# A block with four mixers on one core: value products of the first mixer for four blocks at a time, prefix tiles in its running sum, another order of the weights

## The chip, the cores and the metric

The kernel runs on one core of a Trainium2 chip. The metric is the device time of one execution in microseconds (us); the median over several runs is compared.

## The reference

One transformer-like block over a sequence of 512 tokens of width 1024, all in float32. `x` is normalised and projected by `w_in` to 6,440 columns, which four mixers of width 512 share:

```python
h = _rmsnorm(x, norm_g)
p_fox, p_ssm, p_nsa, p_mem = _split(h @ w_in, ...)
mem_kv = _rmsnorm(mem, mem_norm_g) @ w_mem_kv
o = concat([_fox_mixer(p_fox, ...), _ssd_mixer(p_ssm, ...),
            _nsa_mixer(p_nsa, ...), _mem_mixer(p_mem, mem_kv)])
return _rmsnorm(x + o @ w_out, final_norm_g)
```

- fox (the first mixer): causal attention with 8 heads of 64; to the scores it adds the difference of a running sum over time of the log of a forget gate, `c = cumsum(log_sigmoid(f_logit + f_bias))`; the output is multiplied by a gate.
- ssd (the second): a state-space mixer in four chunks of 128 tokens, behind a convolution over four steps and with a gated norm.
- nsa (the third): attention with compressed, selected and windowed keys, 8 heads in two groups, with a bias by distance.
- mem (the fourth): attention over 256 memory tokens, 4 heads of 128.

## The kernel before

The program is written out by a planner while it is built: Python objects count an estimated clock for each engine, and the order in which instructions are issued follows from it. On the chip the order is fixed.

**The stream of projections.** `ORDER` (line 42) lists 76 weight tiles of 128x1024. Each is loaded by one DMA on SP's queue (the first by two) into a ring of three raw tiles, split by ACT into a rounded high part `wh` and by `tt` (line 500) on DVE or POOL into a low part `wl`; a product in high precision is three matmuls, high by high, high by low and low by high (`three`). `tt` gives the work to DVE only if its estimated end there plus a handicap (`SOON`, `LATER`, `WIDE`) is earlier than on POOL. The first seven tiles (`bv`, `bc`) hold the values and small columns of all four token blocks (`proj_b`, line 554); while the last ones run, the input is normalised. Every further tile of the list is a generator (`tile_a`, line 663, for a projection into the tile `pj`; `out_proj` and `out_last`, lines 824 and 854, for the products with `w_out` into `po`) that stops after every three matmuls. The list is served strictly in order, and `ready` (line 627) says whether its head may start: there must be room in the pools of tiles (`gs`, 51 tiles of 512 columns, and `bs`, 12 of 1024), and an output projection `wo0`, `wo1`, `wo2` needs all four parts of its mixer's output.

**The pipes.** The mixers are pipes of stages (`Pipe`, line 319): `fox` (line 971), `nsa` (1175), `ssm` (1365) and `mem` (1571), with `compress` ("cmp") and `prep` ("pre") as preparations. A step of `fox` or `nsa` is a head pair j and a block b of 128 queries (in `nsa` also a half a); its stages are scores and softmax (s1, tiles `pS`, `pF`, `pN`), transposes (s2, `pT`, `pt`), value products (s3, `pO`) and the gate (s4). `DF, DM, DN, DS` (line 25) say how many steps of a pipe may be in flight, and for each stage a pipe names the PSUM banks and the tiles that it needs. `Sched.run` (line 237 and on) looks at the first `ACTIVE` unfinished pipes in the order of `PIPES`, issues a stage whose data are ready by the estimated clock, and fills PE with the next three matmuls of the list where none is. If the list is blocked, the earliest stage is issued though its data are late.

**The clock.** `Clock.note` (line 123) estimates each instruction. Matmuls of plain fp32 into at most 64 columns use half of the array; between them and all others the estimate adds 100 ns at each change, in either direction.

**The running sum.** `smalls` (line 890) makes the log gates on DVE and writes them into a tile `s4`, four blocks of 128 columns. `fox_bias` (line 925) sums them over time into `pd`: for block t the products of blocks 0 to t-1 with a tile of ones and of block t with a triangle (`U`), which is ten matmuls. A plain fp32 matmul stands as two records in the profile.

**The value products of the first mixer.** In `fox`'s s3 nothing happens for blocks 0 and 2; at block 1 the products of blocks 0 and 1, and at block 3 those of blocks 2 and 3 are issued, into a PSUM tile of which each head of the pair takes 64 rows. The transposed weights (`pt`, one tile of 512 columns for each four blocks of 128 keys of both heads) are held until then.

**The first weight tile.** For the `bv` tiles the six groups of four matmuls (k-half j, part x: 0 high by high, 1 input low, 2 weight low) go in the order (0,0), (0,1), (1,0), (0,2), (1,1), (1,2).

Of the kernel before, what the change touches and what calls it, by code (L numbers as in the profile page):

```python
# [10 lines left out]
FT = mybir.dt.float32  # L11
# [12 lines left out]
NL = 3  # L24
DF, DM, DN, DS = 4, 5, 5, 4
BACKLOG = 3000
RAW, RING = 3, 3
PIPES = "cmp", "fox", "pre", "nsa", "ssm", "mem"
LAST = 3
ACTIVE = 3  # L30

RF, RM, RN, RS = 2, 3, 2, 4

SOON, LATER, WIDE = 500, 2500, 5000

# [6 lines left out]
ORDER = (  # L42
# [14 lines left out]
class Clock:  # L57
# [65 lines left out]
    def note(self, eng, op, a, k):  # L123
# [12 lines left out]
        if eng == "PE":  # L136
# [7 lines left out]
            if tiled != self.tiled:  # L144
                start += 100
                self.tiled = tiled
# [90 lines left out]
class Sched:  # L237
# [53 lines left out]
    def run(self, pipes):  # L291
        self.pipes = pipes = list(pipes)
        while pipes:
# [15 lines left out]
            if best[0] > now:  # L309
                t = self.due()  # L310
                if t <= now or t <= best[0]:
                    if t == math.inf:
                        raise RuntimeError(f"nothing can run: {self.todo[0][0]}, {[p.at for p in pipes]}")
                    self.fill()
                    continue
            best[1].run(self, best[2])

# [42 lines left out]
def block_kernel(ctx, tc, I, out):  # L360
# [26 lines left out]
    def MD(name, w):  # L387
        return sb.tile([128, w], FT, name=name, tag="md", bufs=5)

# [164 lines left out]
    def proj_b(name, n, per, width):  # L554
        pb = [PS("pb") for t in range(4)]
        for i in range(n):
            h_, l_ = get((name, i))
            ks_ = range(i * per, min((i + 1) * per, KT))
            if name == "bv":
                order = [(0, 0), (0, 1), (1, 0), (0, 2), (1, 1), (1, 2)]  # L560
            else:
                order = [(j, x) for j in range(len(ks_)) for x in (0, 1)] + [(j, 2) for j in range(len(ks_))]
# [325 lines left out]
    gat = C1("gat", [128, 4, 24])  # L888

    def smalls():  # L890
        y = SM("y", 64).rearrange("p (t c) -> p t c", t=4)
# [17 lines left out]
        for i in range(4):  # L909
            V.tensor_copy(out=s4f.rearrange("p (t c) -> p t c", t=4)[:, :, 32 * i:32 * i + 8], in_=sp[:, :, 0:8])  # L910
        ea = SM("ea", 8)
        A.activation(ea, v_al, AF.Exp)
# [3 lines left out]
        V.tensor_scalar(out=gat, in0=gat, scalar1=1.0, scalar2=0.5, op0=OP.add, op1=OP.mult)  # L916

    crs = []

# [5 lines left out]
    def fox_bias():  # L925
        s4 = s4f.rearrange("p (t c) -> p t c", t=4)
        p = PS("pd")
        for t in range(4):
            for u in range(t + 1):
                T.matmul(p[:, t * 128:(t + 1) * 128], s4[:, u, :], U if u == t else ones, start=u == 0, stop=u == t)  # L930
        gs.drop()
# [39 lines left out]
    def fox():  # L971
# [28 lines left out]
        def s3(s):  # L1000
            j, b1 = s
            if b1 == 1:
                st["o"] = PS("pO")
            o = st["e", s] = st.get("o")
            for b in (b1 - 1, b1) if b1 % 2 else ():
                pts = st.pop((j, b))
# [168 lines left out]
    def nsa():  # L1175
# [66 lines left out]
        def s3(s):  # L1242
            j, b, a = s
            if a == 0:
                return
            if b == 0 or j == 3 and LAST == 2:
                st["o"] = PS("pO")
            o = st["o"]
            p0, (p1, ct) = [st.pop((j, b, x)) for x in range(2)]
            pa = p0, p1  # L1250
            os_ = [o[64 * x:64 * x + 64, b * 128:(b + 1) * 128] for x in range(2)]
            for x in range(2):
                T.matmul(os_[x], vcm[:, x * 64:(x + 1) * 64], ct[:96], start=True, stop=False)
            for br in range(2):
                for k in range(b + 1):
                    for x in range(2):
                        T.matmul(os_[x], nv[:, k, br * 128 + x * 64:br * 128 + x * 64 + 64], pa[x][br * (b + 1) + k],
                                 start=False, stop=br == 1 and k == b)
            st["e", s] = o
            gs.drop(2 * ((b + 2) // 2))  # L1260

# [66 lines left out]
    def ssm_pre():  # L1328
# [13 lines left out]
        T.matmul(pa[:64, :128], dA2, U, start=True, stop=True)  # L1342
        ar = sb.tile([64, 128], FR, name="ar", tag="md", bufs=5)
        A.copy(out=ar, in_=pa[:64, :128])
# [20 lines left out]
    def ssm():  # L1365
# [147 lines left out]
        def p3(c):  # L1513
            return [("z", j) for j in range(4)], lambda: []

        return Pipe(list(range(4)), [s1, s2, s3, s4, s5], DS, [5, 1, 1, 1, 1], [(2, 0), (1, 0), (2, 0), (0, 0), (3 if LAST == 1 else 1, 0)], RS,
                    {0: p1, 2: p3})
# [157 lines left out]

    bg.until(clock.ready([s4f]))
    cr()
# [116 lines left out]
```

## Time and profile before

| | us |
|---|---|
| median of three runs | 549.83 |
| lowest and highest of them | 547.93, 550.03 |
| the profiled execution | 548.13 |
| its span, first to last instruction | 546.0 |
| TensorE busy | 535.0 (98%) |
| VectorE busy | 326.5 (60%) |
| ScalarE busy | 318.2 (58%) |
| GpSimd busy | 240.1 (44%) |

In the rows below, PE is TensorE's matmuls, PEld its weight loads, DVE VectorE, ACT ScalarE, POOL GpSimd and SP the engine whose queue issues DMAs. Tiles go by the program's names, `out<-in`. Times are from the span's start. Matmuls are pipelined: one lasts longer than the distance to the start of the next, so the pace of a stream is read from starts.

### The profile page before, as it was taken

Reading aid. Unit: us, or ns where it says so; the run is one execution under the profiler, and the core shown is the slowest. Engines: PE = TensorE matmul, PEld = TensorE weight load, DVE = VectorE, ACT = ScalarE, POOL = GpSimd, SP = SyncE. Lnnn points to the kernel's source line nnn. Section 1 sums busy time; section 2 is a strip of 40 time slices with the busy share of each in tenths; the row PEclk is TensorE's granted clock in tenths of the full one; section 3 lists DMA queues with packets and bytes.
Section 4 is the critical chain, followed back from the end, with each engine's and each line's share of the span. In section 5 each row is a group of like instructions: output and inputs, shape, how many; then the busy total and the mean of one; then the engine's idle time right before and its main releaser. Section 6 shows DMA issues by size and latency. Waiting matters only on the chain.

```text
span 546.0 us, 8842 instructions
## 1 busy us (share of the span) xinstructions
PE 535.0 (98%) x3237; PEld 447.8 (82%) x3237; DVE 326.5 (60%) x870; ACT 318.2 (58%) x714; POOL 240.1 (44%) x159
## 2 busy tenths in 40 slices
PE   8999999999999999999999899999999999999995
PEld 5898888887888888888888688888988888888884
DVE  2676678465754536876665755656655576656443
ACT  5755545747766624735553676667666676756333
POOL 3595525325131444767786451133422213055523
PEclk9999999999999999999999999999999999999998
DMA  8774323222441521262326221511421112022113
GB/s 281 303 268 138 116 77 110 83 77 78 141 130 44 199 72 42 100 245 77 116 93 194 76 65 59 161 59 60 155 79 40 68 49 79 1 78 82 73 39 116
DMA packets 18791, 59.01 MB, mean 108 GB/s; under 512 B 2187, under 2 KB 2459, under 8 KB 18748
## 3 DMA queue, kind: packets, MB, share of 16 engines
q1 hardware_dynamic: 18604, 58.19, 31.4%
q8 instruction: 25, 0.41, 0.3%
q10 hardware_dynamic: 144, 0.26, 0.1%
q14 instruction: 18, 0.15, 0.1%
HBM read 55.80 MB, written 4.81 MB: 111 GB/s over the span
## 4 chain that ended last, share of the span: by engine, by line
PE 96%; DMA 1%; ACT 1%; POOL 1%; DVE 0%; SPq 0%; issue 0%; POOLq 0%; ACTq 0%
PE pj L233 47%; PE po L233 16%; PE pO L233 7%; PE pT L233 6%; PE pb L233 6%; PE pS L233 5%; PE pmv L233 2%; PE pW L233 2%; PE pY L233 1%; DMA xt<-in_xT 1%; PE pcm L233 1%; PE pst L233 0%; PE pd L233 0%; PE pR L233 0%; POOL acc L233 0%; PE pG L233 0%
## 5 line engine op out<-in xcount | busy, mean ns | idle before, releaser
L233 POOL TENSOR_TENSOR wl<-raw,wh 128x1024 fp32r<-128x1024 f32 (+1 forms) x72 | 172.1, 2395 | 239.5 <-ACT wh L233 205.8
L233 PE MATMUL pj<-hh,wh 128*128 128x512 f32 x352 | 141.7, 403 | 0.0
L233 PE MATMUL pj<-hh,wl 128*128 128x512 f32 x352 | 137.6, 391 | 0.0
L233 PE MATMUL pj<-hl,wh 128*128 128x512 f32 x352 | 137.4, 390 | 0.0
L233 ACT ACTIVATE wh<-raw 128x1024 fp32r<-128x1024 f32 (+1 forms) x72 | 74.8, 1041 | 14.2 <-DMA raw<-in_wst 8.2
L233 PEld LDWEIGHTS pj<-hh,wl 128*128 128x128 f32 x352 | 66.1, 188 | 14.5
L233 PEld LDWEIGHTS pj<-hh,wh 128*128 128x128 f32 x352 | 66.2, 188 | 12.6 <-issue 1.2
L233 PEld LDWEIGHTS pj<-hl,wh 128*128 128x128 f32 x352 | 66.3, 188 | 11.3
L233 ACT ACTIVATE pN<-pN,nm 128x128 f32<-128x128 f32 (+7 forms) x96 | 45.3, 473 | 29.2 <-DVE nm L233 28.3
L233 PE MATMUL po<-wh,oh 128*128 128x512 f32 x96 | 39.1, 407 | 0.7 <-ACT oh L233 0.7
L233 PE MATMUL po<-wh,ol 128*128 128x512 f32 x96 | 37.6, 392 | 0.6 <-POOL ol L233 0.6
L233 PE MATMUL po<-wl,oh 128*128 128x512 f32 x96 | 37.5, 391 | 0.0
L233 ACT ACTIVATE pN<-pN,rs 128x128 f32<-128x128 f32 (+3 forms) x32 | 18.0, 564 | 25.8 <-DVE rs L233 24.8
L233 DVE CUSTOM_DVE_ANT_0 pN<-pS,bt 128x128 f32<-128x128 f32 (+4 forms) x72 | 21.1, 328 | 18.0 <-PE pS L233 17.7
L233 DVE TENSOR_TENSOR acc<-acc,po 128x512 f32<-128x512 f32 (+1 forms) x33 | 21.2, 666 | 11.1 <-PE po L233 11.0
L233 ACT ACTIVATE pF<-pF,nm 128x128 f32<-128x128 f32 (+3 forms) x32 | 17.8, 556 | 14.3 <-DVE nm L233 14.0
L233 DVE SCALAR_TENSOR_TENSOR xs<-cb,cwh,xs 128x512 f32<-128x512 f32 x24 | 20.7, 861 | 9.0 <-ACT xs L233 8.2
L233 DVE TENSOR_SCALAR rs<-sm 128x3 f32<-128x3 f32 x32 | 8.4, 262 | 28.2 <-ACT pN L233 28.2
L233 PE MATMUL pT<-cst,pN 128*128 128x128 f32 x160 | 23.5, 278 | 1.2 <-ACT pN L233 1.2
L233 ACT COPY pt<-pT 128x512 f32<-128x512 f32 (+1 forms) x43 | 20.6, 485 | 5.8 <-PE pT L233 5.7
L233 PEld LDWEIGHTS pT<-cst,pN 128*128 128x128 f32 x160 | 18.2, 140 | 5.8 <-issue 2.2
L233 PEld LDWEIGHTS po<-wh,ol 128*128 128x128 f32 x96 | 18.0, 188 | 5.0 <-POOL ol L233 1.1
(273 smaller groups left out, 1095.1 us busy)
## 6 DMA issues: line engine op xcount, KB each, us to landing
raw<-in_wst SPq DMA_DIRECT2D x74, 512.0 KB, 3.3
rows<-rv SPq DMA_DIRECT2D x4, 656.0 KB, 7.5
bt<-rows SPq DMA_DIRECT2D x4, 528.0 KB, 4.2
xt<-in_xT SPq DMA_DIRECT2D x8, 256.0 KB, 6.6
xn<-in_xn SPq DMA_DIRECT2D x4, 512.0 KB, 7.8
w<-in_w SPq DMA_DIRECT2D x4, 512.0 KB, 7.2
acc<-in_xn SPq DMA_DIRECT2D x4, 512.0 KB, 5.0
out<-acc SPq DMA_DIRECT2D x7, 256.0 KB, 2.3
```

Source lines behind the costliest of these rows:

```text
L233: return f(*a, **k)
```

## The change

In the first mixer, s3 waits until block `GF - 1` (GF is 4) and issues the products of all four blocks of a head pair in one run; up to eight steps may be in flight. In `smalls`, two adds on DVE make the sums of the first two and the first three blocks of `s4`, in tiles from a pool that grows from five to seven; in `fox_bias` each block then takes one matmul with the triangle and one with ones, seven in all, and the first call waits for these tiles too. The first `bv` tile goes in natural order. The estimate adds 50 ns where a change leads into the half-array matmuls and 220 ns where it leads out. `ssm` comes before `nsa` among the pipes, four of them are looked at, `DM` is 6, `DN` 4, `WIDE` 8000. A stage of `ssm` may ask for three free tiles where it asked for two. When a pipe's best stage has become impossible after the list was looked at, the planner looks again. `nsa`'s s3 is written for a number `GN` of blocks, which is 1 as before. The list of weights has a new order.

```diff
--- before.py
+++ after.py
@@ -22,16 +22,18 @@
 RVW = 656
 WARM = 12
 NL = 3
-DF, DM, DN, DS = 4, 5, 5, 4
+DF, DM, DN, DS = 8, 6, 4, 4
+
+GF, GN = 4, 1
 BACKLOG = 3000
 RAW, RING = 3, 3
-PIPES = "cmp", "fox", "pre", "nsa", "ssm", "mem"
+PIPES = "cmp", "fox", "pre", "ssm", "nsa", "mem"
 LAST = 3
-ACTIVE = 3
+ACTIVE = 4
 
 RF, RM, RN, RS = 2, 3, 2, 4
 
-SOON, LATER, WIDE = 500, 2500, 5000
+SOON, LATER, WIDE = 500, 2500, 8000
 
 TAKES = {"fq": (2, 1), "fk": (2, 1), "fg": (1, 0), "nq": (2, 0), "ng": (1, 0), "z": (1, 0), "mq": (2, 0), "mg": (1, 0),
          "mk": (1, 0), "ks": (0, 4), "kw": (0, 4), "kc": (1, 1), "vc": (1, 1), "xb": (2, 0), "mv": (4, 0),
@@ -40,15 +42,15 @@
 FOX, SSM, NSA, MEM = 0, 2056, 3600, 5416
 
 ORDER = (
-    ("bv", 0), ("bv", 1), ("bv", 2), ("bv", 3), ("bc", 0), ("bc", 1), ("bc", 2), ("vc", 0),
-    ("fq", 0), ("fk", 1), ("xb", 6), ("xb", 4), ("fk", 0), ("xb", 7), ("fk", 3), ("fq", 1),
-    ("fq", 2), ("xb", 1), ("xb", 2), ("fg", 3), ("fg", 0), ("fk", 2), ("kc", 0), ("fg", 1),
-    ("fq", 3), ("fg", 2), ("z", 3), ("z", 0), ("xb", 3), ("xb", 5), ("xb", 0), ("ks", 0), ("z", 1),
+    ("bv", 0), ("bv", 1), ("bv", 2), ("bv", 3), ("bc", 0), ("bc", 1), ("bc", 2), ("fq", 0),
+    ("fg", 1), ("xb", 2), ("fk", 1), ("fq", 2), ("xb", 7), ("fk", 0), ("xb", 5), ("fq", 1),
+    ("xb", 1), ("fg", 3), ("vc", 0), ("xb", 6), ("fk", 3), ("fk", 2), ("fg", 0), ("kc", 0),
+    ("fq", 3), ("fg", 2), ("z", 0), ("z", 3), ("xb", 0), ("xb", 3), ("xb", 4), ("ks", 0), ("z", 1),
     ("z", 2), ("wo0", 0), ("wo0", 1), ("wo0", 2), ("wo0", 3), ("mv", 0), ("mv", 1), ("mv", 2),
-    ("mv", 3), ("nq", 0), ("kw", 0), ("ng", 2), ("wo1", 0), ("wo1", 1), ("mk", 1), ("nq", 1),
-    ("ng", 0), ("wo1", 2), ("wo1", 3), ("nq", 2), ("ng", 1), ("mk", 0), ("mk", 2), ("mk", 3),
-    ("mg", 0), ("ng", 3), ("nq", 3), ("mg", 2), ("mq", 0), ("mq", 1), ("mg", 1), ("mq", 3),
-    ("mq", 2), ("wo2", 0), ("wo2", 1), ("mg", 3), ("wo2", 2), ("wo2", 3), ("wo3", 0), ("wo3", 1),
+    ("mv", 3), ("kw", 0), ("nq", 0), ("ng", 0), ("ng", 1), ("ng", 3), ("wo1", 0), ("wo1", 1),
+    ("nq", 1), ("ng", 2), ("mk", 1), ("wo1", 2), ("wo1", 3), ("nq", 2), ("mg", 3), ("mk", 2),
+    ("mk", 0), ("nq", 3), ("mk", 3), ("mg", 0), ("mq", 0), ("mq", 2), ("mq", 1), ("mq", 3),
+    ("mg", 1), ("wo2", 0), ("wo2", 1), ("mg", 2), ("wo2", 2), ("wo2", 3), ("wo3", 0), ("wo3", 1),
     ("wo3", 2), ("wo3", 3),
 )
 KEYS_A = [k for k in ORDER if k[0] not in ("bv", "bc", "mv") and k[0][:2] != "wo"]
@@ -142,7 +144,7 @@
             if tiled:
                 took /= 2
             if tiled != self.tiled:
-                start += 100
+                start += 50 if tiled else 220
                 self.tiled = tiled
             if start > self.t[eng] + 1700:
                 took += 2000
@@ -313,6 +315,8 @@
                         raise RuntimeError(f"nothing can run: {self.todo[0][0]}, {[p.at for p in pipes]}")
                     self.fill()
                     continue
+                if best[1].due(self, best[2]) == math.inf:
+                    continue
             best[1].run(self, best[2])
 
 
@@ -385,7 +389,7 @@
         return sb.tile([128, w], FT, name=name, tag="sm", bufs=11)
 
     def MD(name, w):
-        return sb.tile([128, w], FT, name=name, tag="md", bufs=5)
+        return sb.tile([128, w], FT, name=name, tag="md", bufs=7)
 
     def PS(name):
         t = ps.tile([128, 512], FT, name=name, tag="ps", bufs=8)
@@ -556,7 +560,9 @@
         for i in range(n):
             h_, l_ = get((name, i))
             ks_ = range(i * per, min((i + 1) * per, KT))
-            if name == "bv":
+            if (name, i) == ("bv", 0):
+                order = [(j, x) for j in range(2) for x in range(3)]
+            elif name == "bv":
                 order = [(0, 0), (0, 1), (1, 0), (0, 2), (1, 1), (1, 2)]
             else:
                 order = [(j, x) for j in range(len(ks_)) for x in (0, 1)] + [(j, 2) for j in range(len(ks_))]
@@ -887,6 +893,8 @@
     dA = C1("dA", [128, 32])
     gat = C1("gat", [128, 4, 24])
 
+    crs, before = [], []
+
     def smalls():
         y = SM("y", 64).rearrange("p (t c) -> p t c", t=4)
         V.tensor_tensor(out=y, in0=nv[:, :, 256:272], in1=v_fd[:, None, :].to_broadcast([128, 4, 16]), op=OP.add)
@@ -908,6 +916,11 @@
         V.scalar_tensor_tensor(out=sp, in0=e, scalar=2.0, in1=y, op0=OP.mult, op1=OP.add)
         for i in range(4):
             V.tensor_copy(out=s4f.rearrange("p (t c) -> p t c", t=4)[:, :, 32 * i:32 * i + 8], in_=sp[:, :, 0:8])
+        s4 = s4f.rearrange("p (t c) -> p t c", t=4)
+        before.append(s4[:, 0, :])
+        for t in (1, 2):
+            before.append(MD("pre", 128))
+            V.tensor_tensor(out=before[t], in0=before[t - 1], in1=s4[:, t, :], op=OP.add)
         ea = SM("ea", 8)
         A.activation(ea, v_al, AF.Exp)
         V.scalar_tensor_tensor(out=dA.rearrange("p (t h) -> p t h", t=4), in0=sp[:, :, 8:16], scalar=-1.0,
@@ -915,8 +928,6 @@
         A.activation(gat, nv[:, :, 272:296], AF.Tanh, scale=0.5)
         V.tensor_scalar(out=gat, in0=gat, scalar1=1.0, scalar2=0.5, op0=OP.add, op1=OP.mult)
 
-    crs = []
-
     def cr():
         if not crs:
             crs.append(fox_bias())
@@ -926,8 +937,9 @@
         s4 = s4f.rearrange("p (t c) -> p t c", t=4)
         p = PS("pd")
         for t in range(4):
-            for u in range(t + 1):
-                T.matmul(p[:, t * 128:(t + 1) * 128], s4[:, u, :], U if u == t else ones, start=u == 0, stop=u == t)
+            T.matmul(p[:, t * 128:(t + 1) * 128], s4[:, t, :], U, start=True, stop=t == 0)
+            if t:
+                T.matmul(p[:, t * 128:(t + 1) * 128], before[t - 1], ones, start=False, stop=True)
         gs.drop()
         c = G("cr", FR)
         A.activation(c, p, AF.Copy, scale=-1.0)
@@ -999,10 +1011,10 @@
 
         def s3(s):
             j, b1 = s
-            if b1 == 1:
+            if b1 == GF - 1:
                 st["o"] = PS("pO")
             o = st["e", s] = st.get("o")
-            for b in (b1 - 1, b1) if b1 % 2 else ():
+            for b in range(b1 + 1 - GF, b1 + 1) if b1 % GF == GF - 1 else ():
                 pts = st.pop((j, b))
                 for k in range(b + 1):
                     for a in range(2):
@@ -1240,24 +1252,24 @@
                 st[s] = (pts, ct)
 
         def s3(s):
-            j, b, a = s
+            j, b1, a = s
             if a == 0:
                 return
-            if b == 0 or j == 3 and LAST == 2:
+            if b1 == GN - 1 or LAST == 2 and (b1 == 0 or j == 3):
                 st["o"] = PS("pO")
-            o = st["o"]
-            p0, (p1, ct) = [st.pop((j, b, x)) for x in range(2)]
-            pa = p0, p1
-            os_ = [o[64 * x:64 * x + 64, b * 128:(b + 1) * 128] for x in range(2)]
-            for x in range(2):
-                T.matmul(os_[x], vcm[:, x * 64:(x + 1) * 64], ct[:96], start=True, stop=False)
-            for br in range(2):
-                for k in range(b + 1):
-                    for x in range(2):
-                        T.matmul(os_[x], nv[:, k, br * 128 + x * 64:br * 128 + x * 64 + 64], pa[x][br * (b + 1) + k],
-                                 start=False, stop=br == 1 and k == b)
-            st["e", s] = o
-            gs.drop(2 * ((b + 2) // 2))
+            o = st["e", s] = st.get("o")
+            for b in ((b1,) if LAST == 2 else range(b1 + 1 - GN, b1 + 1) if b1 % GN == GN - 1 else ()):
+                p0, (p1, ct) = [st.pop((j, b, x)) for x in range(2)]
+                pa = p0, p1
+                os_ = [o[64 * x:64 * x + 64, b * 128:(b + 1) * 128] for x in range(2)]
+                for x in range(2):
+                    T.matmul(os_[x], vcm[:, x * 64:(x + 1) * 64], ct[:96], start=True, stop=False)
+                for br in range(2):
+                    for k in range(b + 1):
+                        for x in range(2):
+                            T.matmul(os_[x], nv[:, k, br * 128 + x * 64:br * 128 + x * 64 + 64], pa[x][br * (b + 1) + k],
+                                     start=False, stop=br == 1 and k == b)
+                gs.drop(2 * ((b + 2) // 2))
 
         def s4(s):
             j, b, a = s
@@ -1340,7 +1352,7 @@
         bg.until(clock.ready([dA2]))
         pa = PS("pa")
         T.matmul(pa[:64, :128], dA2, U, start=True, stop=True)
-        ar = sb.tile([64, 128], FR, name="ar", tag="md", bufs=5)
+        ar = sb.tile([64, 128], FR, name="ar", tag="md", bufs=7)
         A.copy(out=ar, in_=pa[:64, :128])
         V.tensor_tensor(out=ar[32:64], in0=pa[32:64, :128], in1=ar[32:64].bitcast(FT), op=OP.subtract)
         bd = G("bd", FR)
@@ -1513,7 +1525,7 @@
         def p3(c):
             return [("z", j) for j in range(4)], lambda: []
 
-        return Pipe(list(range(4)), [s1, s2, s3, s4, s5], DS, [5, 1, 1, 1, 1], [(2, 0), (1, 0), (2, 0), (0, 0), (3 if LAST == 1 else 1, 0)], RS,
+        return Pipe(list(range(4)), [s1, s2, s3, s4, s5], DS, [5, 1, 1, 1, 1], [lambda c: (max(2, (5, 7, 7, 5)[c] - RS), 0), (1, 0), (2, 0), (0, 0), (3 if LAST == 1 else 1, 0)], RS,
                     {0: p1, 2: p3})
 
     def mem_r():
@@ -1673,7 +1685,7 @@
             continue
         bg.add(key, adders[key[0]](key))
 
-    bg.until(clock.ready([s4f]))
+    bg.until(clock.ready([s4f, *before]))
     cr()
     made = {"fox": fox, "cmp": compress, "mem": mem, "nsa": nsa, "ssm": ssm, "pre": prep}
     bg.run([made[n]() for n in PIPES])
```

## Rows read from the trace of the kernel before

**Rows 1.** The page, first part: busy us, share of the span, instructions.

```profile
PE 535.0 (98%) x3237; PEld 447.8 (82%) x3237; DVE 326.5 (60%) x870; ACT 318.2 (58%) x714; POOL 240.1 (44%) x159
```

**Rows 2.** Waits of PE: waiter, whom for, us in total, times, longest.

```profile
PE pT L233 <- ACT pN L233: 1.2, 1, 1.2
PE po L233 <- ACT oh L233: 0.7, 1, 0.7
```

**Rows 3.** Stretches: length, PE, PEld, DVE, ACT, POOL busy, PE clock, DMA, GB/s.

```profile
89.80:192.80 103.00, 103.00 (x623) 84.72 (x621) 58.23 (x146) 67.27 (x143) 36.53 (x21) 1.00 0.32 109
...
299.40:305.00 5.60, 3.12 (x17) 2.05 (x16) 3.48 (x17) 3.91 (x12) 2.01 (x4) 1.00 0.31 97
305.00:472.00 167.00, 167.00 (x1181) 142.34 (x1182) 100.94 (x406) 111.22 (x305) 51.59 (x36) 1.00 0.23 75
```

**Rows 4.** Groups of PE's instructions, 89.8 to 192.8 us: count, busy, mean ns.

```profile
L233 PE MATMUL pO<-pt,fv 128*64 128x128 f32 x160 | 10.5, 278 | 0.0
```

**Rows 5.** Timeline of PE around one run of value products: start, us, what.

```profile
104.92 0.39 PE L233 MATMUL pj<-hh,wl 128*128 128x512 f32 x1
105.24 0.88 PE L233 MATMUL pO<-pt,fv 128*64 128x128 f32 x12
106.05 0.50 PE L233 MATMUL pj<-hh,wh 128*128 128x512 f32 x1
106.38 0.39 PE L233 MATMUL pj<-hl,wh 128*128 128x512 f32 x1
```

**Rows 6.** Timeline of PE in the running sum.

```profile
53.90 0.38 PE L233 MATMUL pd<-cst,s 128*128 128x128 f32 x2
...
55.24 0.83 PE L233 MATMUL pd<-ones,s 128*128 128x128 f32 x6
55.91 0.39 PE L233 MATMUL pd<-cst,s 128*128 128x128 f32 x2
```

**Rows 7.** Timeline of DVE: the copies into s4, and an add of 128x128.

```profile
51.32 0.44 DVE L233 COPY s<-sp 128x32 f32<-128x32 f32 x4
...
293.55 0.29 DVE L233 TENSOR_TENSOR sq<-sq 128x128 f32<-128x128 f32 x1 [1.01 <-ACT sq L233]
```

**Rows 8.** Timeline of PE in the first weight tile.

```profile
7.29 1.08 PE L233 MATMUL pb<-wh,ul 128*128 128x512 f32 x4
9.04 1.20 PE L233 MATMUL pb<-wh,uh 128*128 128x512 f32 x4 [0.67 <-ACT uh L233]
...
12.80 1.11 PE L233 MATMUL pb<-wh,uh 128*128 128x512 f32 x4
```

**Rows 9.** Timeline of all engines there: low part on POOL, second tile on ACT.

```profile
5.88 1.33 POOL L233 TENSOR_TENSOR wl<-raw,wh 128x512 fp32r<-128x512 f32 x1 [4.62 <-ACT wh L233]
...
11.53 1.05 ACT L233 ACTIVATE wh<-raw 128x1024 fp32r<-128x1024 f32 x1
```

**Rows 10.** Timeline of all engines at PE's wait near 301 us, PE's lines.

```profile
300.99 0.29 PE L233 MATMUL pS<-kl,L 128*128 128x288 f32 x1
...
302.44 0.44 PE L233 MATMUL pT<-cst,pN 128*128 128x128 f32 x2 [1.17 <-ACT pN L233]
...
303.57 0.50 PE L233 MATMUL po<-wh,oh 128*128 128x512 f32 x1 [0.69 <-ACT oh L233]
...
303.91 0.40 PE L233 MATMUL po<-wl,oh 128*128 128x512 f32 x1
...
304.93 0.50 PE L233 MATMUL po<-wh,ol 128*128 128x512 f32 x1 [0.63 <-POOL ol L233]
```

**Rows 11.** The chain that ended last: one projection tile.

```profile
90.43 5.51 PE pj L233 x24
```

**Rows 12.** The instructions on the tile wl: ns min, median, max, first and last start.

```profile
L233 POOL TENSOR_TENSOR wl<-raw,wh x72: 1280/2397/2859, 5.9 to 498.2; 128x1024 fp32r<-128x1024 f32 x70, 128x512 fp32r<-128x512 f32 x2
```

**Rows 13.** Timeline of all engines: a block's first scores and its first transposes.

```profile
124.58 0.40 PE L233 MATMUL pS<-Rk,L 128*128 128x512 f32 x1
...
130.78 1.04 PE L233 MATMUL pT<-cst,pF 128*128 128x128 f32 x8
```

## The prediction

> **What bounds the kernel now.** I read the page's first part, then PE's waits, then the stretches, then PE's timeline wherever a part of the change lands. PE is busy for 535.0 of 546.0 us [rows 1]: the kernel is one stream of matmuls, and a change counts only by what it takes out of that stream, the small breaks inside it included. In the middle of the kernel PE waits at one place alone, 299.4 to 305.0 us, where it works 3.12 of 5.60 us [rows 2, 3]; the stretches of the first mixer (89.8 to 192.8) and of the third (305 to 472) have PE busy from end to end [rows 3]. All granted clocks there are 1.00, so nothing is to be had from the clock. DVE, ACT and POOL are busy for 44 to 60% [rows 1] and matter only as those whom PE waits for.
>
> **The sum's base.** The profiled execution took 548.13 us (span 546.0, 2.1 around it). The three timed runs have a median of 549.83, and spread over 2.1 us; the profiled one is 1.7 below that median. I sum against 548.13 and come back to this below.
>
> **Part by part.**
>
> *Value products of four blocks.* The first mixer's products into 64 columns are 160 records in eight runs of PE's stream now (two per head pair: 12 and 28), and four runs of 40 after [rows 4]. The products themselves stay. What a run costs beside them shows at 104.92 us [rows 5]: the projection before it starts 0.32 us ahead of the next start, where such a matmul passes the stream in 0.23 (0.09 too much); the 12 records take 0.81 us from start to next start, and at the usual 0.055 apiece they should take 0.66 (0.15 too much); and the projection behind again takes 0.33 (0.10 too much). So 0.34 us a run, if a projection follows; where scores or transposes follow, which are plain fp32 too, the last 0.10 is not the run's, since such a group ends with it anyway, and 0.24 is left. Four runs fewer are worth 0.96 to 1.36 us; five of the eight have a projection behind them, so I take 1.2.
>
> *Prefix tiles.* Ten matmuls of the running sum become seven: three of the six against the tile of ones go. Each is two records; six records take 0.67 us of the stream [rows 6]. No wait covers them (PE is in order there), so 0.67 comes off. The two new adds on DVE are of a form that takes 0.29 us each [rows 7], 0.6 together. The four copies that they read end at about 51.8 us and the first product starts at 53.90 [rows 6, 7], since the planner fills with projections until its estimate says that the data are there, and now the estimate includes the adds. Behind them on DVE wait only small tiles that nobody needs for microseconds. I cost them at nothing; the cover is 2 us of projections, and without it they would cost PE 0.6.
>
> *First weight tile in natural order.* PE's second group of four ended its issue at about 8.20 and the third started at 9.04, waiting for ACT's uh of the second input tile [rows 8]: 0.83 us lost. In natural order the third group needs wl of the first half instead, which POOL has by 5.88 + 1.33 = 7.21 [rows 9], so it starts at once, and the stall goes. But what is late next? The second weight tile: ACT makes its wh from 11.53 to 12.58 [rows 9], after the uh that it still has to wait for, and PE comes to it at 12.80 [rows 8], its weight load a little earlier. With 0.83 us less ahead, PE would be there at 11.97 and wait for 12.6 and a weight load of some 0.2. So the stall moves by one tile: the bounds are 0 and 0.83, and I take 0.
>
> *Weight order.* The list is served in order, and the second mixer's output projection (wo1) blocks it until all four of its chunks are done. Now only kw, nq and one gate tile stand between mv and wo1, and at 301 us PE runs dry: in an unbroken stream the scores of 300.99 would pass in 0.13 and the two transposes in 0.22, so the first output product would start at 301.34 and not at 303.57 (2.23 late); the third starts 1.02 us after the second and not 0.23 (0.79 late) [rows 10]. That is 3.0 us. The new list has three gate tiles there, not one. A tile is 24 matmuls and takes 5.5 us [rows 11], so two more give 11 us of cover for a lateness of 3. I take the whole 3.0; the bounds are 3.0 and, if the hole opens elsewhere, nothing.
>
> *The rest.* Pipes in another order: while the second mixer's chunks run, it alone of the pipes has work until the third can start at about 299, so its new rank hardly acts before. Its stages ask for up to one more free tile, which can only delay them; the 11 us stand against that. DN falls from 5 to 4, in a stretch where PE never waits [rows 3]; DM rises. The larger WIDE sends more low parts to POOL, but all 72 pieces are there already [rows 12]. The estimate of 50 and 220 ns moves instructions in PE's order, not their number. The DMAs of the weights are the same in number and size, on SP's queue in another order. All this I cost at nothing, with 1 to 2 us either way for how the pieces fall.
>
> Sum: 1.2 + 0.67 + 0 + 3.0 = 4.9 us off. 548.13 - 4.9 = 543.2 by the profiled execution; by the median, 549.83 - 4.9 = 544.9. Nothing tells which of the two an execution of the new kernel resembles, and I say 544.0.
>
> **The rivals.**
>
> *The hole opens elsewhere.* The list is still served in order, and every blocked head (wo1, wo2, the last gate tiles) can starve PE. For it: one such hole in the kernel before, and a new order of some 40 tiles. Against it: nothing that blocks comes nearer to its producer, and from 305 to 472 PE had no hole at all [rows 3]. It decides if the second mixer ends over 8 us (11 less 3) later against the list. Then 3.0 stays in: 546.2 by the profiled execution, 547.9 by the median.
>
> *The first mixer runs out of tiles: slower.* All four blocks of a pair now hold their transposed weights until the pair's products: six tiles of 512 columns, where the two later blocks held four. By a count from the code, while pair 1 is worked on, the pool of 51 has 16 (normalised input, high and low), 4 (values), 1 (running sum), 12 (queries and keys of pairs 1 to 3), 4 gates, some 6 convolved tiles, the 6, and 4 for scores in work: 53. Then the list may not go on, and PE waits for the pair's own chain, which takes 6.2 us from scores to transposes for the longest block (124.58 to 130.78) [rows 13], now covered by projections. If that happens in each of four pairs with 2 to 4 us uncovered, it costs 8 to 16: 543.2 + 12 = 555. For it: the count, and a gate tile (fg 1) that stands 15 places earlier in the list. Against it: the stretch has PE full from end to end [rows 3], and up to four more blocks may be in flight to fill in. It decides if PE waits for over 5 us in all in that stretch. The Trainium skill (Perfetto Trace Analysis, Optimization Strategy) has a rule that speaks for this rival: a gap that repeats through a stretch on the engine that should be full can mean that there were no buffers for the next tile. No row of the kernel before shows such a gap.
>
> *The first tile's stall really goes.* If the second tile's wh is there earlier than I read, another 0.8 comes off: 542.4.
>
> **How the numbers follow.** Forecast 0.62, hole elsewhere 0.21, tiles run out 0.10, more than the sum (first tile, better packing) 0.07. The range runs from 541.0 (542.4 and a little packing) to 549.0 (the hole elsewhere by the median, 547.9, and 1 us of unlucky packing); outside lie the tiles' rival and some of the last. A measurement of this kernel can tell about 0.5%, 2.7 us: faster is below 547.1, slower above 552.6. The forecast and the last case are faster, of the hole's rival about a quarter (0.05): 0.74. The rest of it is the same, and so is a mild form of the tiles' rival: 0.18. Slower: 0.08.
>
> **What would show it.** Right: 40-record runs of pO in the first mixer, four of them; pd with 14 records over some 1.6 us; no wait of PE of over 0.3 us near 290 to 305; PE's wait at about 8 us gone and one of about 0.7 at 12. Wrong: waits of PE that repeat between 90 and 190 us; a wait in front of po or pT elsewhere; or a PE stream whose records are the same but whose starts lie further apart.

## The result, and the profile after

| us | before | after |
|---|---|---|
| median of four runs | 549.93 | 543.24 |
| lowest and highest | 547.93, 550.49 | 543.04, 544.25 |
| the profiled execution | 548.13 | 544.25 |
| its span | 546.0 | 542.4 |
| TensorE busy | 535.0 | 532.2 |

The ratio is 0.9888 with an interval of 0.9861 to 0.9916, which leaves out 1: 1.1% faster. The forecast was 544.0 in 541.0 to 549.0, so it held, 0.8 us too high. The first line of the page after, against [rows 1]:

```profile
PE 532.2 (98%) x3231; PEld 447.1 (82%) x3231; DVE 334.2 (62%) x878; ACT 317.4 (59%) x710; POOL 237.8 (44%) x157
```

PE has six records fewer (three prefix matmuls of two records) and 2.8 us less to do; the share stays at 98%, since the span shrank as well. The waits of PE after, all of them (waiter, whom for, us in total, times, longest):

```profile
PE pw L235 <- DVE warm L235: 1.3, 1, 1.3
PE pb L235 <- ACT wh L235: 1.3, 2, 0.7
PE pb L235 <- ACT uh L235: 0.8, 1, 0.8
PE pb L235 <- ACT fv L235: 0.3, 1, 0.3
```

Both waits of [rows 2] are gone, and what is left lies in the first 32 us. The three stretches of [rows 3] after (length; PE, PEld, DVE, ACT, POOL busy; PE clock; DMA share; GB/s):

```profile
89.80:192.80 103.00, 103.00 (x598) 85.60 (x596) 60.97 (x152) 66.58 (x141) 33.67 (x15) 1.00 0.33 106
299.40:305.00 5.60, 5.60 (x30) 4.71 (x29) 3.81 (x20) 2.64 (x10) 0.00 (x0) 1.00 0.26 91
305.00:472.00 167.00, 167.00 (x1187) 142.71 (x1186) 106.89 (x406) 112.15 (x304) 51.17 (x36) 1.00 0.23 75
```

The middle one is the row to read: 3.12 of 5.60 us busy before, 5.60 of 5.60 after. PE's timeline of the kernel after, at the places where parts of the change land (start, us, what, and the idle time before it with its releaser):

```profile
8.19 1.07 PE L235 MATMUL pb<-wl,uh 128*128 128x512 f32 x4
10.02 1.19 PE L235 MATMUL pb<-wh,uh 128*128 128x512 f32 x4 [0.76 <-ACT uh L235]
...
13.60 0.98 PE L235 MATMUL pb<-wh,uh 128*128 128x512 f32 x3 [0.56 <-ACT wh L235]
...
44.61 0.39 PE L235 MATMUL pj<-hh,wh 128*128 128x512 f32 x1
...
55.51 0.60 PE L235 MATMUL pd<-cst,s 128*128 128x128 f32 x4
...
57.06 0.31 PE L235 MATMUL pa<-dA,cst 128*128 128x32 f32 x2
...
125.14 2.40 PE L235 MATMUL pO<-pt,fv 128*64 128x128 f32 x40
127.48 0.39 PE L235 MATMUL pS<-Rk,L 128*128 128x256 f32 x1
127.70 0.28 PE L235 MATMUL pS<-Rl,M 128*128 128x256 f32 x1
127.82 0.28 PE L235 MATMUL pS<-Rk,L 128*128 128x256 f32 x1
...
535.61 0.28 PE L235 MATMUL po<-lh,ol 128*128 128x256 f32 x1
```

Four such runs of 40 value products stand in this timeline (at 125, 148, 171 and 193 us). The running sum now takes 57.06 - 55.51 = 1.55 us, where it took 2.15 (from 53.90 [rows 6] to the next start at 56.05). In this execution the inputs came late (PE waits at 10.02 and again at 13.60), and the first projection starts at 44.61. The first projection and the last matmul of the profiled execution of before:

```profile
43.69 0.39 PE L233 MATMUL pj<-hh,wh 128*128 128x512 f32 x1
...
539.47 0.28 PE L233 MATMUL po<-lh,ol 128*128 128x256 f32 x1
```

From the first projection to the last matmul it is 491.0 us after (44.61 to 535.61) and 495.8 before: 4.8 less, where the sum had 4.9.

**Why the medians differ by more than that.** The medians lie 6.7 us apart, and the stretch above explains 4.8 of it. The trace of an experiment whose matmuls stand in the same order around the hole (`b_first`, below) shows where another part goes. PE's timeline there, right behind the hole at 301 us:

```profile
304.90 0.55 PE L233 MATMUL po<-wh,ol 128*128 128x512 f32 x1 [0.62 <-POOL ol L233]
305.24 0.63 PE L233 MATMUL po<-wh,oh 128*128 128x512 f32 x1
305.67 0.63 PE L233 MATMUL po<-wl,oh 128*128 128x512 f32 x1
...
308.65 0.39 PE L233 MATMUL po<-wh,ol 128*128 128x512 f32 x1
308.88 0.39 PE L233 MATMUL po<-wh,oh 128*128 128x512 f32 x1
```

and the same kernel's stretch from 305 us (columns as above):

```profile
305.00:309.00 4.00, 4.00 (x11) 3.18 (x12) 3.17 (x9) 2.51 (x8) 4.00 (x2) 0.57 0.00 0
```

Eight matmuls run 0.43 us apart instead of 0.23, which costs 1.6 us, and the granted clock over the stretch is 0.57, so for most of it at the lower of its two levels (1.2 GHz). What PE did before is the hole: 3.12 us of work in 5.60. The profiled execution of before has the same hole and no such stretch behind it (clock 1.00 from 305 us on, [rows 3]). From the first projection to the last matmul b_first takes 497.4 us (43.66 to 541.02), 1.6 more than before's 495.8.

How often that happens can be read, with care, from the mean granted clock of the other executions. The clock also falls behind the last matmul, where it costs PE nothing; in the profiled execution of before (columns as above):

```profile
542.20:546.00 3.80, 0.00 (x0) 0.00 (x0) 0.15 (x1) 0.12 (x1) 0.00 (x0) 0.50 0.37 138
```

That fall alone can bring the mean to 0.996 (`a_first_old`, below), and both falls together stand as 0.994 in b_first. In the three sets of experiments the kernel before was run 37 times. Of these, 26 have a mean clock below 0.996, and their median is 549.62; four have 0.999, and their median is 548.06, which is 1.6 lower, as in the two traces. The other seven, at 0.996 (median 548.65), can be of either kind. Read so, the hole costs 3.0 us in itself and, in most executions, 1.6 more. Closing the hole and opening it again bears this out: all four executions of `b_cover` have a mean clock of 0.997 to 0.998, all ten of `a_nocover` one of 0.992 to 0.995 (both below).

A last 0.3 us lies outside the span: the 37 executions of before took 2.1 to 2.2 us more than their spans, the four of after 1.7 to 1.9. Why is open. Together 4.8 + 1.6 + 0.3 = 6.7, the difference of the medians; the start of the stream, which varies by over 1 us between the traces, is left out of this.

Without the hole the times scatter less: 543.04 to 544.25. The Trainium skill (TensorE: Matmul & The Clock Gate, HAM oscillation) says that an idle gap of PE can bring the clock back to half rate, paid by the matmuls behind it. The trace of b_first agrees (0.57 over the 4 us behind the hole), though PE was not idle through the hole but in pieces; the trace of before, with the same hole, kept 1.00.

### The profile page after: what moved, and what is told of

Its sections match the earlier page's. It is cut to its first block, busy times and chain, and to the rows that moved or that the text cites. A ratio compares the mean times of both kernels' runs of the same rounds, so it can differ in the third digit from the quotient of the medians.

```text
span 542.4 us, 8826 instructions
## 1 busy us (share of the span) xinstructions
PE 532.2 (98%) x3231; PEld 447.1 (82%) x3231; DVE 334.2 (62%) x878; ACT 317.4 (59%) x710; POOL 237.8 (44%) x157
## 4 chain that ended last, share of the span: by engine, by line
PE 96%; DMA 1%; ACT 1%; SPq 1%; POOL 0%; DVE 0%; issue 0%; POOLq 0%
PE pj L235 47%; PE po L235 16%; PE pO L235 7%; PE pT L235 6%; PE pS L235 5%; PE pb L235 5%; PE pmv L235 2%; PE pW L235 2%; DMA xt<-in_xT 1%; PE pY L235 1%; PE pcm L235 1%; SPq L235 1%; PE pst L235 0%; PE pR L235 0%; PE prs L235 0%; POOL acc L235 0%
## 5 line engine op out<-in xcount | busy, mean ns | idle before, releaser
L235 DVE TENSOR_SCALAR rs<-sm 128x3 f32<-128x3 f32 x32 | 10.7, 334 | 28.1 <-ACT pN L235 28.1
L235 DVE SCALAR_TENSOR_TENSOR xs<-cb,cwh,xs 128x512 f32<-128x512 f32 x24 | 19.0, 790 | 13.9 <-ACT xs L235 13.4
L235 DVE COPY pt<-pT 128x512 f32<-128x512 f32 (+1 forms) x36 | 21.0, 590 | 2.3 <-PE pT L235 2.0
```

The lines of the kernel that those rows point to most:

```text
L235: return f(*a, **k)
```

## Experiments

All ratios are to the kernel before on the same chip (medians there: 549.51, 548.67 and 549.63 us for the three sets).

### The cover alone: `b_cover`

The kernel before, two gate tiles more ahead of wo1, nothing else.

```diff
-    ("mv", 3), ("nq", 0), ("kw", 0), ("ng", 2), ("wo1", 0), ("wo1", 1), ("mk", 1), ("nq", 1),
-    ("ng", 0), ("wo1", 2), ("wo1", 3), ("nq", 2), ("ng", 1), ("mk", 0), ("mk", 2), ("mk", 3),
+    ("mv", 3), ("nq", 0), ("kw", 0), ("ng", 2), ("ng", 0), ("ng", 1), ("wo1", 0), ("wo1", 1), ("mk", 1), ("nq", 1),
+    ("wo1", 2), ("wo1", 3), ("nq", 2), ("mk", 0), ("mk", 2), ("mk", 3),
```

> The kernel before, with two gate tiles of the third mixer moved ahead of wo1 in the list, nothing else. Theory (the wait near 301 us is missing cover): 3.0 us off, 545 to 547, no wait of PE over 0.3 us between 200 and 470 us. Rival (a list served in order opens the hole elsewhere): within 1 us of before, with a wait ahead of po, pT or pO elsewhere.

Measured: 545.51 us, ratio 0.9925 (0.9907 to 0.9943), 4.0 off. Of PE's waits behind the start one is left:

```profile
PE pO L233 <- ACT ct L233: 0.4, 1, 0.4
```

The hole closes and opens nowhere else to speak of. The first projection and the last matmul:

```profile
43.75 0.39 PE L233 MATMUL pj<-hh,wh 128*128 128x512 f32 x1
...
537.17 0.28 PE L233 MATMUL po<-lh,ol 128*128 128x256 f32 x1
```

That is 493.4 us, 2.4 less than in the profiled execution of before, whose clock held. The new wait takes 0.4 of the gain back, so closing the hole was worth 2.8 of the 3.0 that were read from the timeline. The medians differ by 4.0, which is 2.4 and the 1.6 of the clock. So two tiles moved in the list bring 4.0 of the 6.7 us of the whole change.

### The cover taken out of the new kernel: `a_nocover`

The kernel after, one gate tile ahead of wo1 instead of three.

```diff
-    ("mv", 3), ("kw", 0), ("nq", 0), ("ng", 0), ("ng", 1), ("ng", 3), ("wo1", 0), ("wo1", 1),
+    ("mv", 3), ("kw", 0), ("nq", 0), ("ng", 0), ("wo1", 0), ("wo1", 1), ("ng", 1), ("ng", 3),
```

> The changed kernel, with one gate tile and not three ahead of wo1, the other two behind it. Theory (cover): the wait ahead of po comes back, 2 to 4 us slower than the changed kernel, 545 to 548. Rival (it was the new rank of the second mixer or the other estimate that closed it): within 1 us of the changed kernel, no wait ahead of po.

Measured: 551.4 us, ratio 1.0032 (1.0022 to 1.0042), 8.2 above the kernel after. Waits of PE, and the stretch behind the longest of them (columns as in [rows 3]):

```profile
PE pT L235 <- ACT pN L235: 4.3, 1, 4.3
...
PE pO L235 <- DVE ct L235: 1.2, 1, 1.2
PE po L235 <- POOL wl L235: 0.5, 1, 0.5
```

```profile
305.00:309.00 4.00, 4.00 (x23) 3.12 (x23) 3.06 (x10) 3.70 (x11) 3.38 (x2) 0.73 0.00 0
```

The hole is back in front of wo1, larger than in the kernel before (4.3 us in one piece, from 299.3), with a lower clock behind it (0.73) and two new waits near 362 and 365 us. So the cover is needed in the new order too; at 2 to 4 us the size was expected too small.

### Value products of four blocks alone: `b_group`

```diff
-DF, DM, DN, DS = 4, 5, 5, 4
+DF, DM, DN, DS = 8, 5, 5, 4
+
+GF = 4
...
-            if b1 == 1:
+            if b1 == GF - 1:
...
-            for b in (b1 - 1, b1) if b1 % 2 else ():
+            for b in range(b1 + 1 - GF, b1 + 1) if b1 % GF == GF - 1 else ():
```

> The kernel before, with the first mixer's value products in four runs of 40 records and eight steps in flight, nothing else. Theory (change of the array's shape costs 0.24 to 0.34 us a run): 1.0 to 1.4 us off, no wait of PE between 90 and 190 us. Rival (the pool of tiles runs out): waits of PE that repeat there, 5 us slower or more.

Measured: 554.52 us, ratio 1.009 (1.0072 to 1.0108): 5.0 slower. The first mixer's stretch and the one behind it (columns as in [rows 3]), and the waits of PE that are new in the second:

```profile
90.00:225.00 135.00, 135.00 (x823) 112.23 (x823) 74.55 (x182) 82.69 (x170) 52.84 (x31) 1.00 0.30 99
225.00:300.00 75.00, 68.51 (x401) 56.18 (x400) 45.23 (x95) 32.60 (x67) 49.93 (x40) 0.98 0.31 106
```

```profile
PE pst L235 <- DVE xde L235: 2.7, 2, 1.8
...
PE prs L235 <- POOL rsr L235: 1.2, 1, 1.2
PE pmv L235 <- POOL ml L235: 0.9, 1, 0.9
```

Where the longer-held weights lie, PE is never short (135.00 of 135.00). It is short 6.5 us in the stretch just behind: 3.9 in the second mixer (pst and prs) and 2.5 in the mv tiles of the list (pmv). The hole at 301 us is closed in this kernel (5.60 of 5.60 us busy from 299.4), so the new waits cost more than the 5.0. In the stretch behind, the first products of wo0 start at 237.6 us, 4.7 later than before (232.9), while the second mixer's second chunk starts 16 us earlier: its exponentials, which ACT makes from pR and which begin at 250.4 before, begin at 234.2. By the code that chunk takes tiles of the same pool of 51, and the list's head must then wait for room. That the pool was spent by a chunk that ran ahead is the likely cause; it is read from the order of events and the code, not tried by itself. The grouping in the old list and estimate costs more than it gives.

### One tile less: `b_ng50`

The kernel before, with a pool of 50 tiles.

```diff
-    NG, NB = 51, 12
+    NG, NB = 50, 12
```

> The kernel before with 50 tiles of 512 columns in its pool and not 51, nothing else. Theory (the list is blocked where the pool is full, and the order of the whole rest follows): waits of PE in the second mixer's stretch from 225 to 300 us as in the kernel before with longer runs, 4 us or more slower than before. Rival (the pool has slack, and the waits of that kernel come from the longer runs themselves): within 1 us of before.

Measured: 577.67 us, ratio 1.0506 (1.0478 to 1.0534): 28 slower. The two largest of its waits, and the stretch of the third mixer's end:

```profile
PE pT L233 <- ACT pN L233: 9.5, 4, 3.3
PE pT L233 <- ACT pM L233: 4.1, 3, 1.9
```

```profile
460.00:500.00 40.00, 28.26 (x203) 23.49 (x201) 20.62 (x87) 21.00 (x64) 0.66 (x4) 0.83 0.04 14
```

One tile less costs 28 us, so the pool has no slack in the kernel before; 4 us or more had been expected. Part of it lies where the tiles are short (from 225 to 300 us PE works 68.60 of 75.00), and more at the end of the third mixer, where PE waits in front of transposes with nothing of the list to fill in, at a clock of 0.83.

### The estimate, and the list without it: `a_est`, `b_order`

The first is the kernel after with the old estimate, the second the kernel before with the new list alone.

```diff
-                start += 50 if tiled else 220
+                start += 100
```

> The changed kernel with the old estimate of a change of the array's shape (100 ns both ways); list, products and sums as changed. Theory of the prediction (the estimate moves instructions, and costs nothing): within 1 us of the changed kernel. Rival (the list fits one order alone: with the old estimate its tiles are used up early and wo2 blocks it while the third mixer still works): waits of PE between 450 and 495 us, 4 to 10 us slower than the changed kernel.

> The kernel before with the new list of weights alone. Theory of the prediction (three gate tiles ahead of wo1 close the wait): 3.0 us off, 545 to 547. Rival (the new list alone moves the waits to wo2): no wait near 301 us, but waits of PE between 450 and 495 us, and no faster than before, 549 to 556.

Measured: a_est 557.88 us, ratio 1.0157 (1.0136 to 1.0178), 14.6 above the kernel after; b_order 558.64 us, ratio 1.0184 (1.0167 to 1.02), 10 above the kernel before. PE's timeline of a_est at the end of the third mixer:

```profile
454.79 0.40 PE L235 MATMUL pj<-hh,wl 128*128 128x512 f32 x1
...
474.01 0.44 PE L235 MATMUL pO<-ct,vcm 96*64 96x128 f32 x4 [1.81 <-ACT ct L235]
...
479.67 0.44 PE L235 MATMUL pO<-ct,vcm 96*64 96x128 f32 x4
...
487.72 0.63 PE L235 MATMUL po<-wh,oh 128*128 128x512 f32 x1
```

Its stretch from 456 to 474 us, and b_order's:

```profile
456.00:474.00 18.00, 13.25 (x75) 10.28 (x74) 11.42 (x54) 12.19 (x37) 0.00 (x0) 0.72 0.01 2
```

```profile
456.00:474.00 18.00, 13.51 (x86) 10.93 (x84) 11.65 (x56) 12.68 (x40) 0.18 (x1) 0.83 0.01 2
```

Between 454.79 and 487.72 not one matmul of the list runs: its head is wo2, which needs the last output of the third mixer, and that pair's products start at 479.67 (in the kernel after at 465.42). With nothing to fill, PE waits in front of most steps for the softmax on ACT, works 13.25 of 18.00 us, and the granted clock falls to 0.72 on top. Both kernels show the same picture (in b_order the projections end at 457.42): the new list with the old estimate gives PE its projections too early, and has none left at the end. In size both lie above what was expected of them (4 to 10 us for a_est, at most 556 for b_order). So the new list does not work without the new estimate; the new estimate alone in the kernel before was not run. What the two do to each step of the planner was not followed further.

### The first weight tile: `b_first`, `a_first_old`

The natural order alone in the kernel before, and the old order in the kernel after.

```diff
-            if name == "bv":
+            if (name, i) == ("bv", 0):
+                order = [(j, x) for j in range(2) for x in range(3)]
+            elif name == "bv":
```

> The kernel before, with the first weight tile in natural order, nothing else. Theory (the stall moves to the second weight tile): within 0.2 us of before, a wait for ACT's wh of 0.5 to 0.8 us near 12 us in place of the one for uh near 8 us. Rival (the stall goes): 0.8 us off, no wait near 12 us.

> The changed kernel with the first weight tile in the old order; no other matmul moves. Theory (the stall only moves): within 0.2 us of the changed kernel. Rival (natural order is worth its stall): 0.6 to 0.9 us slower.

Measured: b_first 549.59 us, ratio 0.9994 (0.9979 to 1.0008); a_first_old 543.11 us, ratio 0.9896 (0.9881 to 0.991), 0.1 from the kernel after. PE's timeline of b_first:

```profile
8.90 1.21 PE L233 MATMUL pb<-wh,uh 128*128 128x512 f32 x4
...
12.68 1.20 PE L233 MATMUL pb<-wh,uh 128*128 128x512 f32 x4 [0.72 <-ACT wh L233]
```

The wait of [rows 8] at 9.04 is gone and stands again at 12.68, for the second tile's wh, with 0.72 us: nothing gained. In the kernel after the first of the two waits did not always go: PE still stands 0.76 us in front of uh at 10.02 there, 0.38 in a_same and none in a_cut (both below), besides the wait of 0.56 to 0.58 for the second tile's wh in all three.

### The runs cut in two again: `a_cut`

The kernel after, with projections let in between the second and the third block, so that the 12 and 28 records of before come back.

```diff
             for b in range(b1 + 1 - GF, b1 + 1) if b1 % GF == GF - 1 else ():
+                if b == 2:
+                    bg.fill()
```

> The changed kernel with three matmuls of the list put into the middle of each run of 40 value products (behind blocks 0 and 1), so that there are eight runs again; the order elsewhere stays nearly the same. Theory (a change of the array's shape costs 0.24 to 0.34 us a run, on the stream): 1.0 to 1.4 us slower than the changed kernel. Rival (the gain came from deeper packing, not from the runs): within 0.3 us.

> The changed kernel itself, for comparison with the next two on the same chip. Both theories: 543 to 544, ratio to before 0.988 to 0.990.

Measured on the same chip: 544.72 us for a_cut, ratio 0.9912 (0.9891 to 0.9933), and 543.2 for the kernel after itself (a_same, ratio 0.9885, 0.9862 to 0.9908): 1.5 for four runs more. PE's timeline of a_cut:

```profile
123.97 0.88 PE L235 MATMUL pO<-pt,fv 128*64 128x128 f32 x12
124.78 0.50 PE L235 MATMUL pj<-hh,wh 128*128 128x512 f32 x1
125.11 0.39 PE L235 MATMUL pj<-hl,wh 128*128 128x512 f32 x1
125.34 0.40 PE L235 MATMUL pj<-hh,wl 128*128 128x512 f32 x1
125.67 1.75 PE L235 MATMUL pO<-pt,fv 128*64 128x128 f32 x28
127.35 0.38 PE L235 MATMUL pS<-Rk,L 128*128 128x256 f32 x1
```

The 12 take 0.81 from start to next start and the 28 take 1.68, 2.49 in all, where the 40 in one run of the kernel after take 2.34 (0.15 more). Of the projections between the two runs, the first takes 0.33 instead of 0.23 (0.10 more, behind a run), and so does the last, which starts at 125.34 (0.10 more, ahead of one). That is 0.35 by the rows, and by the whole 0.37 a run: from the first of these products to the last matmul a_cut is 1.47 us longer. The upper bound of the prediction was 0.34. All six executions of a_cut (544.50 to 545.43) lie above all six of a_same (543.09 to 544.36). All four of its cuts are filled with projections.

### The stall that moved, taken out: `a_split`, `a_split2`

In the kernel after ACT makes the second tile's wh behind the uh of the fourth input tile, and that input lands late. Here it goes ahead of it; PE's order is the same.

```diff
-        if k in (0, 3):
+        if k in (0, 2):
             split(1 if k == 0 else 2)
```

> The changed kernel with ACT's high part of the second weight tile made one input tile earlier. Theory (in natural order the stall sits in that high part alone): the wait for wh near 12 us goes, 0.4 to 0.9 us off the changed kernel. Rival (the input tiles' landing sets the start either way): the wait for uh takes its place, within 0.2 us.

> The changed kernel with ACT's high part of the second weight tile one input tile earlier, again, beside the changed kernel on the same chip. Theory (the moved stall goes): 0.4 to 0.9 us faster than the changed kernel. Rival (the landing of the inputs sets the start): within 0.2 us.

Measured: a_split 542.76 us, ratio 0.9888 (0.9872 to 0.9904); a_split2, the same kernel beside a_same, 542.6 us, ratio 0.987 (0.9848 to 0.9893), 0.6 below a_same. ACT's timeline of a_same and of a_split2:

```profile
11.44 0.72 ACT L235 ACTIVATE uh<-xt,vec 128x512 fp32r<-128x512 f32 x1 [1.24 <-DMA xt<-in_xT]
12.07 1.04 ACT L235 ACTIVATE wh<-raw 128x1024 fp32r<-128x1024 f32 x1
```

```profile
9.97 1.06 ACT L235 ACTIVATE wh<-raw 128x1024 fp32r<-128x1024 f32 x1 [0.58 <-DMA raw<-in_wst]
```

In a_same ACT stands 1.24 us in front of the fourth input before it comes to the raw tile; in a_split2 it takes the raw tile as soon as that lands (a wait of 0.58). With wh 2.1 us earlier, PE's wait for it (0.58 us at 13.16 in a_same) is gone in the traces of both a_split and a_split2. (The wait for uh, 0.38 us in a_same, is gone as well; as a_cut has none either, this is not shown to come from the edit.) The gain of 0.6 us is small and the two intervals of the ratios overlap, but all five executions of a_split2 (542.06 to 542.92) lie below all six of a_same (543.09 to 544.36). It is the fastest version of all.

## Why the prediction held, and where it did not

- **The weight order (3.0) was right for the hole, and the hole was not the whole of it.** In b_cover closing it was worth 2.8 at full clock. The step "All granted clocks there are 1.00, so nothing is to be had from the clock" failed: it was true of the profiled execution, while in most others, by their mean clock, the hole lowers the clock behind it for another 1.6 us. This fits what the prediction noted and could not explain, that the profiled execution stood 1.7 below the median. By the median, 549.83 - 4.9 would have been 544.9; it came out at 543.2. The forecast of 544.0 was the middle between the two sums, and no row spoke for the middle; that it lies only 0.8 off is in part luck, since the 1.6 of the clock and the 0.3 outside the span stood in no term.
- **The value products (1.2) were about right, by a reading that was not.** "Five of the eight have a projection behind them" is four by the trace of before; behind two runs stand scores and behind two transposes. "Where scores or transposes follow, which are plain fp32 too" does not hold for scores: behind a run the first score takes 0.22 where the next takes 0.12 (127.48, 127.70 and 127.82 in the kernel after), so scores pay for the run as projections do. a_cut measures 1.5 for four cuts filled with projections, over the upper bound of 1.36. With 0.37 a run, and 0.10 less for the two runs in front of transposes, the change would save about 1.3 (an estimate from a_cut and these rows); no run measures it alone in a kernel that is otherwise undisturbed, since b_group brings waits of its own.
- **The prefix tiles (0.67)** show 0.60 in the starts of the trace, and no wait beside them. They were not tried alone.
- **The first weight tile (0)** was right in place and size: the stall appeared at the second tile's wh, 0.72 us in b_first, and the old order in the kernel after costs nothing (543.11). The sign "PE's wait at about 8 us gone" held in b_first and a_cut, not in the profiled execution of after, where 0.76 us of it stood at 10.02. Its other bound, that the stall goes for good, needed one more edit, a_split.
- **The rest at nothing** was right only as a sum: 3.0, 0.6 and about 1.3 make 4.9, and the stretch from the first projection to the last matmul is 4.8 shorter. The step "the estimate of 50 and 220 ns moves instructions in PE's order, not their number" is true and says nothing of cost: the order decides when the list runs out, and with the new list the old estimate costs 14.6 us. The new list alone costs 10 in the old kernel, the grouping alone 5. The 1 to 2 us either way that the prediction allowed hold only for parts that were fitted to each other, and nothing in its working showed that these were. The other parts of the rest (the order of the pipes, how many are looked at, the tiles a stage may ask for, WIDE, DM, DN) were not tried.
- **The rivals.** The hole did not open elsewhere in the kernel after. It does as soon as the list is changed without the estimate: at the end of the third mixer, in front of wo2, where the prediction argued from [rows 3] that PE had no hole. The rival of the tiles did not come about in the kernel after (103.00 of 103.00 in the first mixer's stretch). By b_ng50 its premise, a pool without slack, is right; its place was not: in b_group PE is short behind the pairs, not in them. The consistent gap that the Trainium skill (Perfetto Trace Analysis, Optimization Strategy) takes as a sign of too few buffers shows in no run between 90 and 225 us; where tiles were short, the waits were few, different and later (b_ng50: nothing from 90 to 225 us, then 9.5 us in four waits in front of pT).

## What to carry to other kernels

Where a planner fixes the order, its list, its estimate and its limits hang together, so judge them together. Here the whole list, the grouping or a tile less, each alone, cost 5 to 28 us, while a move of two tiles aimed at one hole that had been read in the timeline brought 4.0 by itself. Price a hole in TensorE's stream by what is missing in it and by the pace of the matmuls behind it, and look at more than one execution before you call the clock full. A mean clock over a whole execution also counts what happens behind the last matmul. When a stall has only moved, look for what stands in front of the work that is late: here it was not slow, it stood behind an input that it did not need.

## What was not expected of the hardware

- A hole of some 3 us in TensorE's work (3.12 busy of 5.60 us) was followed in one execution by eight matmuls at 0.43 us apiece, in another by none: the same order of matmuls, the granted clock 0.57 and 1.00 over the next 4 us.
- Stretches in which TensorE worked three quarters of the time in short pieces had a granted clock of 0.72 (13.25 of 18.00 us) and 0.83 (13.51 of 18.00; 28.26 of 40.00), so the work between short waits ran slower as well. In a_est the clock is 0.50 from 459.3 to 469.5 us with PE busy for 8.67 of 10.20; the waits between 455 and 488 us add up to 7.5 us, and the kernel is 14.6 slower than the kernel after.
